# Four rows of each partition of block 4 loaded from GpSimd's queue while the first blocks are stored

## The chip, the cores and the metric

The kernel runs on one core of a Trainium2 chip. The metric is the device time of one execution in microseconds (us); the median of several executions is compared. The core has five engines that run side by side (PE, the matrix engine; DVE, the vector engine; ACT, the scalar engine; POOL, which is GpSimd; SP, the sync engine) and sixteen DMA engines that move data between the chip's main memory (HBM) and the on-chip memory (SBUF, 128 partitions). SP, ACT and GpSimd can each issue transfers on a queue of their own; every transfer is cut up over DMA engines, and each engine that takes part adds to the transfer's semaphore when its part has landed. Sixteen means that all has landed.

## The reference

The computation is a linear layer with a weight that is normalised by column (DoRA). x is 16 x 2048 x 256, so 32768 rows of 256 numbers; all inputs and outputs are float32.

```python
W_adapted = W + scale * (lora_A @ lora_B)                 # 256 x 256, rank 16
W_norm = np.sqrt(np.sum(W_adapted ** 2, axis=0, keepdims=True) + 1e-8)
W_final = W_adapted / W_norm * m
y = x.reshape(-1, 256) @ W_final
```

32 MiB of x are read and 32 MiB of y are written. The weights are small.

## The kernel before, in words

The 32768 rows are eight blocks of 4096. A block lies in SBUF as 128 partitions of 32 rows (1 KB a row), so that a partition's part of a block is one run of 32 KB in HBM. There are five block buffers (`x_bufs`, `XBUFS = 5`): blocks 0 to 4 have a buffer each, and blocks 5 to 7 reuse the buffers of blocks 0 to 2, once those have been stored. Results are written back in place: the product of a piece of x overwrites that piece, and the store reads from the same buffer.

The unit of work is the group `g`: four rows of each partition (`J = 4`), so eight groups make a block (`CH = 8`), and there are 64 groups. Two groups make a pair `p`, 32 in all. For each pair, GpSimd casts x to bf16 (L208), PE transposes it (L321), DVE copies the transposes out of PSUM (L248), PE multiplies by the final weight (L335), and ACT copies each group's product back into the x buffer (L276).

Transfers follow two lists that are written out by hand, `loads` and `stores`, whose entries are (first group, number of groups, rows of each partition in one transfer), with the group after which a store is due as a fourth number. `transfer` (issuing line L146) issues an entry:

- SP issues all loads in the order of the list. Blocks 0 to 3 come first, then 24 of the 32 rows of block 4, all of it in the first 5 us. Then SP waits for store 0 to land, issues the last 8 rows of block 4 as two transfers of four rows, and goes on with two loads of half a block each for block 5. It waits for store 1 before the second half of the sequence (block 6), and for stores 2 and 3 before block 7.
- ACT issues the stores. Store 0 (block 0) is due only after group 19, store 1 (block 1) after group 20, stores 2 and 3 (block 2, 12 and 20 rows) after group 24. The stores of block 3's first five groups are cut in five transfers of four rows; the later ones are larger again.
- GpSimd issues no transfer. At pair 15 (`REST = 15`) it waits until store 2 has landed, before it casts on. PE, DVE and ACT depend on its casts, so that they rest too.

At a cast GpSimd waits for the load that brings the pair's groups, but only where the group before came with another load. A partition's rows of a load or store form one run of bytes, so a load of 24 rows moves runs of 24 KB, one of 4 rows runs of 4 KB.

H is the first group of block 5 (40), so `H - CH` is the first of block 4 (32). At the end, SP waits for the late stores, which closes the program (L360).

Of the kernel before, what the change touches and what calls it, by code (L numbers as in the profile page):

```python
# [11 lines left out]
def kernel(  # L12
# [10 lines left out]
    nc = tc.nc  # L23
    P = 128
# [5 lines left out]
    x_flat = x.flatten_outer_dims()  # L30
    out_flat = out.flatten_outer_dims()
    N, IN = x_flat.shape
# [3 lines left out]
    J = 4  # L36
    DJ = 32
# [5 lines left out]
    XBUFS = 5  # L43
    CH = DJ // J
# [4 lines left out]
    NXB = 2  # L49

    REST = 15
    NXT = 2
    F8 = 2 * J * P

# [7 lines left out]
    def sb(name, shape, dtype):  # L62
        return ctx.enter_context(nc.sbuf_tensor(name, shape, dtype))
# [4 lines left out]
    x_bufs = [sb(f"x_sb{k}", [P, DJ, IN], FP32) for k in range(XBUFS)]  # L68
    xb_bufs = [sb(f"xb{k}", [P, 2 * J, IN], BF16) for k in range(NXB)]
    xt_bufs = [sb(f"xt{k}", [P, F8, KC], BF16) for k in range(NXT)]  # L70
    w_nat = sb("w_nat", [P, KC, OUT], FP32)
# [38 lines left out]
    H = XBUFS * CH  # L110
    loads = [(0, 2, 2 * J), (2, 2, 2 * J), (4, 4, 4 * J)]
    loads += [(b * CH, CH, CH * J) for b in range(1, XBUFS - 1)]
    loads += [(H - CH, 6, 6 * J), (H - 2, 2, J)]
    loads += [(g0, 4, 4 * J) for g0 in range(H, NCH, 4)]
    load_of = {g: n for n, (g0, cnt, _) in enumerate(loads) for g in range(g0, g0 + cnt)}
    stores = [(b * CH, CH, CH * J, 19 + b) for b in range(F - 1)]
# [7 lines left out]
    def pieces(entry):  # L124

        return 16 * (entry[1] * J // entry[2])
# [5 lines left out]
    def sem(name):  # L132
        if name not in sems:
            sems[name] = tc.alloc_semaphore(name)
        return sems[name]

    def transfer(engine, name, entry, dram, store):
        g0, cnt, rows = entry[:3]
        b, c = divmod(g0, CH)
        (u0, ucnt), = [u for u in units if u[0] <= g0 < u[0] + u[1]]  # L140
        unit = dram[u0 * J * P : (u0 + ucnt) * J * P].rearrange("(p j) k -> p j k", p=P)
        for r in range(0, cnt * J, rows):
            here = x_bufs[b % XBUFS][:, c * J + r : c * J + r + rows, :]
            there = unit[:, (g0 - u0) * J + r : (g0 - u0) * J + r + rows, :]
            src, dst = (here, there) if store else (there, here)
            engine.dma_start(out=dst, in_=src).then_inc(sem(name), 16)  # L146

    def load_x(n):
        transfer(nc.sync, f"load{n}", loads[n], x_flat, False)

    def store_y(n):
        transfer(nc.scalar, f"store{n}", stores[n], out_flat, True)

    def wait_load(engine, g):
        engine.wait_ge(sem(f"load{load_of[g]}"), pieces(loads[load_of[g]]))

    def wait_store(engine, n):
        engine.wait_ge(sem(f"store{n}"), pieces(stores[n]))
# [3 lines left out]
        out=w_nat[:], in_=W.rearrange("(p t) o -> p t o", t=KC)  # L162
    ).then_inc(sem("load_w"), 16)
    nc.scalar.dma_start(
        out=a_nat[:], in_=lora_A.rearrange("(p t) r -> p t r", t=KC)
# [2 lines left out]
    nc.scalar.dma_start(out=m_row[:], in_=m[None, :]).then_inc(sem("load_m"), 16)  # L168
    for n in range(len(loads)):

        if loads[n][0] == H - 2:
            wait_store(nc.sync, 0)
        if loads[n][0] == H + CH:
            wait_store(nc.sync, 1)
        if loads[n][0] == H + 2 * CH:
            wait_store(nc.sync, 2)
            wait_store(nc.sync, 3)
        load_x(n)
# [5 lines left out]
        out=identity[:],  # L184
        in_=zeros[:],
# [7 lines left out]
    for p in range(1, NPR):  # L193
        b, c = divmod(p, PRB)
        for g in (2 * p, 2 * p + 1):
            if g == 2 or load_of[g - 1] != load_of[g]:
                wait_load(nc.gpsimd, g)


        if p == 1:  # L200
            nc.gpsimd.wait_ge(sem("dve"), 6)
        if p == 2:
            nc.gpsimd.wait_ge(sem("dve"), 8)
        if p == REST:
            wait_store(nc.gpsimd, FIRST - 2)
        if p >= NXB:
            nc.gpsimd.wait_ge(sem("turned"), p - NXB + 1)
        nc.gpsimd.tensor_copy(  # L208
            out=xb_bufs[p % NXB][:],
            in_=x_bufs[b % XBUFS][:, 2 * c * J : 2 * (c + 1) * J, :],  # L210
        ).then_inc(sem("rounded"), 1)
# [14 lines left out]
        out=wa[:], in0=ab_ps, scalar=float(scale), in1=w_nat[:], op0=ALU.mult, op1=ALU.add  # L226
# [19 lines left out]
    for p in range(NPR):  # L246
        nc.vector.wait_ge(sem("turned"), p + 1)
        nc.vector.tensor_copy(  # L248
            out=xt_bufs[p % NXT][:].rearrange("p r t -> p (r t)").bitcast(FP32),
            in_=xt_ps[p % 2][:],  # L250
# [4 lines left out]
    for engine, idle in ((nc.gpsimd, 8), (nc.vector, 24)):  # L255
# [13 lines left out]
        out=norm[:], in_=n2_ps, func=AF.Sqrt, bias=eps_col[:]  # L269
    ).then_inc(sem("act"), 1)  # L270
    drains = 0
    for g in range(NCH):
        b, c = divmod(g, CH)
        nc.scalar.wait_ge(sem("product"), g + 1)

        nc.scalar.copy(  # L276
            out=x_bufs[b % XBUFS][:, c * J : (c + 1) * J, :], in_=y_ps[g % 2][:]
        ).then_inc(sem("room"), 1)
        due = [n for n in range(len(stores)) if stores[n][3] == g]
        if due:  # L280
            drains += 1
            nc.scalar.drain().then_inc(sem("done"), 1)  # L282
            nc.scalar.wait_ge(sem("done"), drains)
            for n in due:
                store_y(n)
# [42 lines left out]
    def product(p):  # L328
        take("copied")
        for h in range(2):  # L330
            take("room")
            for t in range(KC):
                for j in j_order:
                    r = (h * J + j) * P
                    i = nc.tensor.matmul(  # L335
                        y_ps[h][:, j, :],
                        xt_bufs[p % NXT][:, r : r + P, t],
                        w_final[:, t, :],
# [57 lines left out]
```

## Time and profile before

| what | us |
|---|---|
| median of 9 runs | 162.9 |
| lowest and highest of them | 162.46, 163.8 |
| the profiled execution's own time | 163.03 |
| its span, first to last instruction | 161.7 |
| PE busy | 96.9 |
| ACT busy | 66.0 |
| GpSimd busy | 60.7 |
| DVE busy | 45.0 |
| DMA, mean over the span | 417 GB/s, 67.43 MB |
| GpSimd's wait for store 2 | 23.5 |

The span is that of the program's instructions on the core; 1.3 us of the profiled execution's time lie outside it. Busy times are sums over the span. In the rows of DMA queues, q1 is SP's and q10 is ACT's. The profile also gives, for each of 40 slices of the span, how busy the sixteen DMA engines were on average, and its trace keeps every DMA packet (queue, start, length, bytes) and the time of every semaphore step, without the number of the DMA engine.

### The profile page before, as it was taken

What the parts mean: (1) busy time and instruction counts of PE and PEld (TensorE: products, weight loads), DVE (VectorE), ACT (ScalarE), POOL (GpSimd) and SP (SyncE); (2) the same over time, 40 slices, a digit from 0 to 9 for tenths busy, and PEclk for the clock granted to TensorE, in tenths of its full rate; (3) what the DMA queues carried; (4) which work ended last, traced back from release to release, by engine and by line L of the source; (5) the groups of instructions that cost most, each with busy time, mean ns of one, the idle gap of its engine ahead of it and who ended that gap; (6) DMA issues with size and microseconds to landing.
All of it is one profiled execution on the core that took longest, in us unless ns stands there. A gap on an engine that the chain in (4) does not pass through costs nothing. (4 is left out here: it accounts for less than half of the span.)

```text
span 161.7 us, 2027 instructions
## 1 busy us (share of the span) xinstructions
PE 96.9 (60%) x786; PEld 84.8 (52%) x786; DVE 45.0 (28%) x44; ACT 66.0 (41%) x68; POOL 60.7 (38%) x38
## 2 busy tenths in 40 slices
PE   1596936999997940000899999999895940000000
PEld 0285925899996920000789999878775930000000
DVE  0567321245353330000334444443442300000000
ACT  3321740576866560000067777577572850000000
POOL 1045319476776000003955944944909300000000
PEclk9999995799999995555599999999999998555555
DMA  4999999999999999989999999999999999999994
GB/s 164 420 454 462 389 502 405 389 511 397 421 389 486 389 502 410 438 363 443 392 422 419 412 444 431 414 440 433 413 468 411 470 415 405 472 413 413 430 425 199
DMA packets 4645, 67.43 MB, mean 417 GB/s; under 512 B 657, under 2 KB 674, under 8 KB 1698
## 3 DMA queue, kind: packets, MB, share of 16 engines
q1 hardware_dynamic: 2304, 33.82, 49.0%
q10 hardware_dynamic: 2338, 33.59, 48.9%
q14 instruction: 3, 0.02, 0.0%
HBM read 33.85 MB, written 33.55 MB: 417 GB/s over the span
## 5 line engine op out<-in xcount | busy, mean ns | idle before, releaser
L276 ACT COPY x_sb<-y_ps 128x1024 f32<-128x1024 f32 x64 | 62.2, 1014 | 60.0 <-PE y_ps L335 57.4
L208 POOL CAST xb<-x_sb 128x2048 bf16<-128x2048 f32 x31 | 58.2, 1893 | 65.0 <-DMA x_sb<-in_x_dram 30.7
L335 PE MATMUL y_ps<-w_final,xt 128*128 128x256 bf16 x512 | 64.2, 280 | 4.2 <-PEq L311 4.2
L248 DVE COPY xt<-xt_ps 128x1024 f32<-128x1024 f32 x32 | 39.1, 1224 | 76.3 <-PE xt_ps L321 76.2
L335 PEld LDWEIGHTS y_ps<-w_final,xt 128*128 128x128 bf16 x512 | 51.3, 101 | 12.1 <-issue 5.4
L321 PE MATMUL xt_ps<-identity,xb 128*128 128x128 f32 x264 | 37.7, 291 | 24.9 <-PEq L311 24.7
L321 PEld LDWEIGHTS xt_ps<-identity,xb 128*128 128x128 f32 x264 | 32.5, 151 | 27.1 <-issue 26.6
L264 ACT CAST xb<-x_sb 128x2048 bf16<-128x2048 f32 x1 | 1.9, 1898 | 2.7 <-DMA x_sb<-in_x_dram 2.7
L292 PE MATMUL y_ps<-identity,a_nat 128*16 128x128 f32 x2 | 0.6, 394 | 3.5 <-DMA a_nat<-in_lora_A_dram 3.5
L262 ACT ACT_TABLE_LOAD x1 | 1.3, 1283 | 2.4 <-issue 2.4
L238 DVE RECIPROCAL rnorm<-norm 128x256 f32<-128x256 f32 x1 | 1.8, 1754 | 1.3 <-ACT norm L268 1.3
L305 PE MATMUL y_ps<-sq,ones 128*128 128x256 f32 x4 | 2.1, 674 | 0.0
L292 PEld LDWEIGHTS y_ps<-identity,a_nat 128*16 128x16 f32 x2 | 0.1, 88 | 3.5 <-issue 3.5
L301 PE MATMUL y_ps<-m_row,ones 1*128 1x256 f32 x2 | 1.2, 710 | 1.1 <-DMA m_row<-in_m_dram 1.1
L214 POOL MEMSET xb<- 128x2048 bf16 x1 | 1.8, 1804 | 0.0
L305 PEld LDWEIGHTS y_ps<-sq,ones 128*128 128x128 f32 x4 | 1.2, 326 | 0.8 <-DVE sq L229 0.7
L301 PEld LDWEIGHTS y_ps<-m_row,ones 1*128 1x128 f32 x2 | 0.5, 308 | 1.6 <-DMA m_row<-in_m_dram 1.6
L220 DVE CAST b_bf<-b_nat 16x256 bf16<-16x256 f32 x1 | 0.3, 282 | 2.8 <-DMA b_nat<-in_lora_B_dram 2.8
L268 ACT ACTIVATE norm<-y_ps,eps_col 128x256 f32<-128x256 f32 x1 | 0.5, 474 | 1.2 <-PE y_ps L305 1.2
L296 PE MATMUL y_ps<-b_bf,aT 16*128 16x256 bf16 x2 | 0.6, 404 | 0.6 <-DVE aT L222 0.6
L225 DVE SCALAR_TENSOR_TENSOR wa<-y_ps,w_nat 128x512 f32<-128x512 f32 x1 | 0.7, 692 | 0.8 <-PE y_ps L296 0.8
L241 DVE TENSOR_TENSOR w_final<-wam,rnorm 128x256 bf16<-128x256 f32 x2 | 0.8, 421 | 0.0
(14 smaller groups left out, 3.7 us busy)
## 6 DMA issues: line engine op xcount, KB each, us to landing
out_dram<-x_sb ACTq DMA_DIRECT2D x5, 4096.0 KB, 28.6
x_sb<-in_x_dram SPq DMA_DIRECT2D x7, 2048.0 KB, 30.6
x_sb<-in_x_dram SPq DMA_DIRECT2D x3, 4096.0 KB, 30.1
out_dram<-x_sb ACTq DMA_DIRECT2D x2, 2048.0 KB, 29.4
x_sb<-in_x_dram SPq DMA_DIRECT2D x1, 3072.0 KB, 46.1
out_dram<-x_sb ACTq DMA_DIRECT2D x2, 1536.0 KB, 19.4
out_dram<-x_sb ACTq DMA_DIRECT2D x1, 2560.0 KB, 29.6
out_dram<-x_sb ACTq DMA_DIRECT2D x5, 512.0 KB, 36.9
```

Of the source, the lines that this page charges most:

```text
L208: nc.gpsimd.tensor_copy(out=xb_bufs[p % NXB][:], in_=x_bufs[b % XBUFS][:, 2 * c * J : 2 * (c + 1) * J, :],).then_inc(sem("rounded"), 1)
L214: nc.gpsimd.memset(xb_bufs[NPR % NXB][:], 0.0).then_inc(sem("rounded"), 1)
L238: nc.vector.reciprocal(out=rnorm[:], in_=norm[:]).then_inc(dv, 1)
L241: i = nc.vector.tensor_mul(out=w_final[:, t], in0=wam[:, t], in1=rnorm[:])
L248: nc.vector.tensor_copy(out=xt_bufs[p % NXT][:].rearrange("p r t -> p (r t)").bitcast(FP32), in_=xt_ps[p % 2][:],).then_inc(sem("copied"), 1)
L262: nc.scalar.activation(out=warm[:], in_=eps_col[:], func=AF.Sqrt)
L264: nc.scalar.copy(out=xb_bufs[0][:], in_=x_bufs[0][:, 0 : 2 * J, :]).then_inc(sem("early"), 1)
L276: nc.scalar.copy(out=x_bufs[b % XBUFS][:, c * J : (c + 1) * J, :], in_=y_ps[g % 2][:]).then_inc(sem("room"), 1)
L301: nc.tensor.matmul(mb_ps, ones[0:1, :], m_row[:], start=True, stop=True).then_inc(pe, 1)
L305: i = nc.tensor.matmul(n2_ps, ones[:], sq[:, t, :], start=(t == 0), stop=(t == KC - 1))
L321: i = nc.tensor.transpose(xt_ps[p % 2][:, j * P : (j + 1) * P], xb_bufs[p % NXB][:, j, :].bitcast(FP32), identity[:],)
L335: i = nc.tensor.matmul(y_ps[h][:, j, :], xt_bufs[p % NXT][:, r : r + P, t], w_final[:, t, :], start=(t == 0 and (j % (J // 2)) == 0), stop ...
```

## The change

The load of block 4 is shortened from 24 rows of each partition to 20. The next four rows (20 to 23) are loaded by GpSimd, in three transfers that are issued just before its wait at pair 15: one for partitions 0 to 5, one for partitions 6 to 125, one for partitions 126 and 127 (`SHARES`). The last eight rows are loaded by SP as before, as two transfers of four rows behind its wait for store 0, now with the semaphore `short`. GpSimd waits for `side` and `short` in full before it casts pair 18, whose second group holds rows 20 to 23; before, there was no wait at pair 18, and the eight rows were waited for at pair 19. The groups 37 to 39 are in no entry of `loads` any more, hence the guard with `in load_of`.

```diff
+    SIDE = 4
+    SHORT = 4
+    SHARES = ((0, 6), (6, 120), (126, 2))
...
-    loads += [(H - CH, 6, 6 * J), (H - 2, 2, J)]
+    loads += [(H - CH, 5, 5 * J)]
...
+    def load_end(engine, name, p0, cnt, r, rows, **kw):
+
+        unit = x_flat[(H - CH) * J * P : H * J * P].rearrange("(p j) k -> p j k", p=P)
+        engine.dma_start(
+            out=x_bufs[XBUFS - 1][p0 : p0 + cnt, r : r + rows, :],
+            in_=unit[p0 : p0 + cnt, r : r + rows, :],
+            **kw,
+        ).then_inc(sem(name), 16)
...
-        if loads[n][0] == H - 2:
+        if loads[n][0] == H:
             wait_store(nc.sync, 0)
+            for r in range(5 * J + SIDE, DJ, SHORT):
+                load_end(nc.sync, "short", 0, P, r, SHORT)
...
-            if g == 2 or load_of[g - 1] != load_of[g]:
+            if g in load_of and (g == 2 or load_of.get(g - 1) != load_of[g]):
                 wait_load(nc.gpsimd, g)
...
         if p == REST:
+            for k, (p0, cnt) in enumerate(SHARES):
+                load_end(
+                    nc.gpsimd, "side", p0, cnt, 5 * J, SIDE, max_dma_last_dim=SIDE * IN
+                )
             wait_store(nc.gpsimd, FIRST - 2)
+        if 2 * p < H - 3 <= 2 * p + 1:
+            nc.gpsimd.wait_ge(sem("side"), 16 * len(SHARES))
+            nc.gpsimd.wait_ge(sem("short"), 16 * ((3 * J - SIDE) // SHORT))
```

GpSimd's program gains the three transfers; the instructions of the other engines, and their order, are the same, but for the widths of SP's loads of block 4.

## The prediction

> **What bounds the kernel now.** I read the page first (DMA rows, queues, chain that ended last), then busy time by stage, then the order of time around the change, then the DMA issues, and last the trace's records of single DMA packets and of each semaphore's sixteen landings.
>
> ```profile
> span 161.7 us, 2027 instructions
> DMA  4999999999999999989999999999999999999994
> q1 hardware_dynamic: 2304, 33.82, 49.0%
> q10 hardware_dynamic: 2338, 33.59, 48.9%
> PE y_ps L335 3%; PE xt_ps L321 2%; ACT x_sb L276 1%; ACTq L282 1%
> ```
>
> The two queues (q1: loads from SP; q10: stores from ACT) fill 97.9% of sixteen engines' span. The chain of instructions is short, because the last 29 us hold none: only stores drain. So the time is the bytes at the DMA engines' rate, plus any moment in which an engine has nothing to do, plus the lateness of the engine that ends last. By stages (the last two columns are the DMA share and GB/s):
>
> ```profile
> 12.90:47.70 34.80, 29.29 (x246) 26.32 (x246) 13.59 (x12) 19.37 (x20) 20.93 (x12) 0.90 1.00 433
> 60.00:75.50 15.50, 0.00 (x0) 0.00 (x0) 0.00 (x0) 0.89 (x1) 0.00 (x0) 0.54 0.99 422
> 75.50:90.00 14.50, 12.43 (x96) 11.10 (x97) 4.90 (x4) 6.49 (x7) 10.29 (x6) 0.79 1.00 414
> 140.00:159.00 19.00, 0.00 (x0) 0.00 (x0) 0.00 (x0) 0.00 (x0) 0.00 (x0) 0.50 1.01 434
> 159.00:160.00 1.00, 0.00 (x0) 0.00 (x0) 0.00 (x0) 0.00 (x0) 0.00 (x0) 0.50 0.31 131
> 160.00:161.00 1.00, 0.00 (x0) 0.00 (x0) 0.00 (x0) 0.00 (x0) 0.00 (x0) 0.50 0.12 49
> 161.00:161.70 0.70, 0.00 (x0) 0.00 (x0) 0.00 (x0) 0.00 (x0) 0.00 (x0) 0.50 0.00 0
> ```
>
> One queue alone runs at 433 to 434 GB/s; loads and stores mixed, at 422 and 414. From 160 to 161 us the share is 0.12, about two engines of sixteen: two are late, and the span waits for them. The packet records say how late. Each engine has eight packets per full transfer and then a 4-byte packet for the semaphore; on one engine the next packet starts 3 to 4 ns before the last one ends, so each engine's sequence can be followed. The last semaphore packets end at 159.4 to 160.2 us on fourteen engines, at 160.79 on one (the second late engine) and at 161.36 on one (the late engine). The late engine was level with the others at 49.6 us, 0.6 us behind at 69.7, 1.3 at 84 and 1.7 at the end. The second got its 1.15 in two stores of 32 KB packets: 0.37 at 49 to 60 us, 0.48 at 123.8 to 131.5 (six packets of 1.27 to 1.32 us where 1.213 is usual), the rest in pieces.
>
> ```profile
> 47.74 0.37 ACTq L146 DMA_DIRECT2D out_dram<-x_sb  x1
> 50.11 1.90 POOL L208 CAST xb<-x_sb 128x2048 bf16<-128x2048 f32 x1 [0.73 <-PE xt_ps L321]
> 75.53 3.73 POOL L208 CAST xb<-x_sb 128x2048 bf16<-128x2048 f32 x2 [23.53 <-DMA out_dram<-x_sb]
> 83.31 1.89 POOL L208 CAST xb<-x_sb 128x2048 bf16<-128x2048 f32 x1 [1.84 <-PE xt_ps L321]
> 60.06 26.78 SPq L146 DMA_DIRECT2D x_sb<-in_x_dram  x8
> ```
>
> Store 0 is issued at 47.74. GpSimd ends pair 14 at 52.0 and then sits 23.5 us for store 2. Pair 18 is cast at 83.31. SP issues nothing between 4.7 and 60.06, where store 0 has landed.
>
> ```profile
> x_sb<-in_x_dram SPq DMA_DIRECT2D x1, 3072.0 KB, 46.1
> out_dram<-x_sb ACTq DMA_DIRECT2D x1, 4096.0 KB, 12.3
> out_dram<-x_sb ACTq DMA_DIRECT2D x1, 2048.0 KB, 29.3
> ```
>
> The load that the change shortens lands 46.1 us after its issue (50.34 us): it is the last thing in q1. The last store waits: its issue is 29.3 us before its landing and it needs 4.9, so some 24 us lie between compute and the end.
>
> **The change part by part.**
>
> *Load of block 4: 20 rows in place of 24.* Per engine eight packets of 24 KB (0.916 us each) become eight of 20 KB (0.763, between that and the 0.761 of 20 KB stores): 1.22 us less in q1. Engines ended this load at 49.45 to 49.88 us (median 49.62) and passed straight to store 0. They will end it at 48.24 to 48.67, median 48.40.
>
> *The join to store 0.* Store 0's issue doesn't move: its products come from blocks 0 to 2. When can its first packet start? The row: the first ACT issue began at 0.90 us, on empty rings, and its first packet started at 1.93, 1.03 us later; so 47.74 + 1.03 = 48.77. Every engine is then idle from its end of load to 48.77: 0.37 us at the median. The Trainium skill, "DMA: Bandwidth & Descriptors", Specifications, gives about 0.6 us to the first byte for the hardware path: store 0 could start at 48.35, and the hole closes to nothing at the median. I take the trace's 1.03; the other end stays for the range. After the join all engines start together, 0.89 us earlier than before at the median, 0.88 on the late engine, 0.69 on the second (it ended its load at 49.46).
>
> *Three transfers on GpSimd.* They issue after pair 14, at 52.0, and lie in the 23.5 us wait, so GpSimd pays nothing for them; with some us per issue they would still fit. If that cover were gone, compute would move by it, and has the 24 us above. Their 128 pieces of 4 KB cost 0.159 us each (4 KB loads of before). Spread evenly that is 8 x 0.159 = 1.27 per engine against 1.22 saved: +0.05, and three semaphore packets of 0.009. The sum over all engines is kept; what changes is who does it. No queue of GpSimd's is in the trace. The skill (same page, "Why a DMA increments its semaphore by 16 and not by 1") says that a GpSimd transfer is cut over the largest count up to 16 that divides its outer size, on consecutive engines from a cursor that goes round. With the cursor at engine 0 at the start: 6 partitions go to engines 0 to 5, 120 go as 15 shares of 8 to engines 6 to 15 and 0 to 4, 2 go to 5 and 6. Engine 5, the sixth, gets 2 pieces and the others 8 or 9. The same section states an exception, direct copies that use sixteen shares with partitions/16 rounded up: then 120 partitions fill engines 0 to 14, and it is the sixteenth that is spared. I take the first, since only it fits what the shares 6, 120, 2 add up to; the second is a rival.
>
> Ends of the engines, against before:
> - the late engine, if it is the sixth: 161.36 - 0.88 + 2 x 0.159 + 0.03 = 160.83
> - the second: 160.79 - 0.69 + 8 or 9 x 0.159 + 0.03 = 161.40 to 161.56
> - a typical one: 159.6 - 0.89 + 1.30 to 1.46 = 160.0 to 160.2.
>
> So the second late engine ends last: +0.04 to +0.20 us against 161.36. Had store 0 started at 48.35 this would be -0.3 to -0.2.
>
> *A third queue beside the stores.* SP's first short load was issued at 60.06 and had its first packet at 64.15[...]; so GpSimd's begin near 57 and, one 0.159 packet after each 1.213 one, last eight or nine turns of 1.37: to about 69. Before, mixing began at 64. Seven more microseconds mixed, at the price of the row of 60 to 75.5 (422 for 433, 2.5%), is 0.18 us; the row of 75.5 to 90 (414, 4.4%) would make 0.31, and small packets read beside large writes may cost nothing, as 90 to 121 us ran at 435: 0 to 0.31, and I take 0.1.
>
> *The moved waits.* The two short loads still follow store 0, on SP, as many and as large (512 KB each); store 0 starts 0.89 earlier and carries two or three extra packets, so SP moves by -0.5 us or so. The new wait at pair 18 is for GpSimd's and the short loads. Before, the short loads landed at 73.1 and 79.4; pair 18 is cast at 83.31: 4 us of cover. Behind that wait are all later casts, and behind them PE, ACT and the stores; without cover it would eat of the 24 us and not lengthen the run.
>
> Sum: +0.04 to +0.20, plus 0.1: **+0.2 us**. Made on the profiled execution (span 161.7, own time 163.03), which is 0.13 over the median of 162.9: so 163.1. A run of this kernel can be told from no change from about 0.3%, 0.49 us.
>
> **The rivals.**
>
> *A: the share misses the late engine.* By the exception, because the cursor stands elsewhere at launch, or because the late engine isn't the sixth. The late engine then takes 8 or 9 pieces too: 161.36 - 0.88 + 1.30 to 1.46 = 161.78 to 161.94, +0.4 to +0.6, with mixing +0.5 to +0.7: slower, 163.4 to 163.6. The trace numbers no engines, so nothing in it says that the late one is the sixth; it decides as soon as fewer than about 3 pieces are spared there. For: the hole at the join is paid by all. Against: by the cursor rule the shares spare exactly one engine, and the trace has one that is later than all the others.
>
> *B: the third queue stalls the engines.* The trace has such stalls where stores and loads are mixed: at 68.3 three packets of 1.213 took 1.34, 1.62 and 1.74, and the 20 KB stores of 77 to 84 us lost 6.8 us together, 0.42 per engine. A second such episode and slow descriptors of GpSimd: +0.8 to +1.5, 163.7 to 164.4. Against: at 90 to 121 us mixing costs nothing.
>
> *C: faster.* The second engine's lateness is one execution's accident, and the late engine's is not: the stalls of the second come in two stores alone. Then the late engine ends last at 160.83, with mixing 160.9: -0.4; with store 0's first packet at 48.35 as well, -0.8. 162.1 to 162.5. For: the fastest run of before is 162.46, so lateness does vary.
>
> **How the numbers follow.** My forecast 0.42, A 0.27, B 0.10, C 0.21. Within 0.3% lie 0.32 of the forecast, 0.05 of A and 0.02 of C: 0.39. Slower: 0.07 of the forecast, 0.22 of A, B: 0.39. Faster: 0.03 of the forecast and 0.19 of C: 0.22. Range 162.2 to 164.0: it leaves out the best of C and the worst of B. The forecast's own range is 162.6 to 163.5.
>
> **What would show it.** Right: a dip of the DMA row at 48.3 to 48.8 us; a third queue of about 0.52 MB between 57 and 70; pair 18 still held by PE and not by a DMA; after 159 us one or two engines left over, with less than the 2.0 us (159.38 to 161.36) that lie between the first ender and the last before. Wrong: no dip (C's half); an engine that still ends 1.5 us after the others (A); a new stretch below 415 GB/s at 57 to 75 us (B); the span below 161.2 or above 162.2.

## The result, and the profile after

The changed kernel takes 163.79 us (median of 10 executions, 163.26 to 164.16), the kernel before 162.89 (31 executions). The ratio is 1.0055, with a 95% interval of 1.0041 to 1.0070: slower by about 0.9 us. Timed once more beside other kernels it was 163.91 against 162.74, ratio 1.0079 (1.0053 to 1.0106).

The execution with the profile was one of the longer ones of this kernel, 164.9 us. So I read three traces of the changed kernel: this one, a second (163.89) and a third (163.72). From the page of the first (DMA busy, rates, queues; q0 is GpSimd's):

```profile
span 163.6 us, 2030 instructions
DMA  4999998999999999989999999999999999999992
DMA packets 4853, 67.43 MB, mean 412 GB/s; under 512 B 737, under 2 KB 754, under 8 KB 1906
q10 hardware_dynamic: 2338, 33.59, 48.8%
q1 hardware_dynamic: 2304, 33.29, 47.8%
q0 software_dynamic: 208, 0.52, 0.8%
```

The bytes are the same and the engines are as busy, but they moved 412 GB/s in place of 417. There is no dip at 48 us. The stages (last columns: DMA share, GB/s) say where the rate went:

```profile
12.90:47.70 34.80, 29.27 (x252) 26.61 (x253) 14.33 (x12) 19.44 (x21) 21.70 (x12) 0.95 1.01 434
52.00:60.00 8.00, 5.16 (x46) 4.29 (x44) 2.45 (x2) 4.76 (x5) 1.20 (x2) 0.99 1.02 426
60.00:75.50 15.50, 0.00 (x0) 0.00 (x0) 0.00 (x0) 0.00 (x0) 0.00 (x0) 0.50 0.98 404
75.50:90.00 14.50, 10.98 (x80) 9.64 (x81) 3.67 (x3) 5.42 (x6) 9.41 (x5) 0.72 1.01 412
160.00:161.00 1.00, 0.00 (x0) 0.00 (x0) 0.00 (x0) 0.00 (x0) 0.00 (x0) 0.50 0.35 147
161.00:162.00 1.00, 0.00 (x0) 0.00 (x0) 0.00 (x0) 0.00 (x0) 0.00 (x0) 0.50 0.15 66
162.00:163.00 1.00, 0.00 (x0) 0.00 (x0) 0.00 (x0) 0.00 (x0) 0.00 (x0) 0.50 0.12 49
```

Up to 47.7 us the rate does not differ. In 60 to 75.5 us it is 404 GB/s where it was 422; the third trace has 404 too, but the second has 424, and its execution was as long as the median:

```profile
60.00:75.50 15.50, 0.00 (x0) 0.00 (x0) 0.00 (x0) 0.00 (x0) 0.00 (x0) 0.50 1.01 424
```

So the lower rate of this stage is not the whole loss. At the end a tail of two engines (share 0.12) lasts until 163, two microseconds later than before. In order of time around the change:

```profile
46.98 0.37 ACTq L152 DMA_DIRECT2D out_dram<-x_sb  x1
51.18 2.03 POOL L160 DMA_DIRECT2D x_sb<-in_x_dram  x3
76.98 3.73 POOL L234 CAST xb<-x_sb 128x2048 bf16<-128x2048 f32 x2 [23.78 <-DMA out_dram<-x_sb]
85.16 1.89 POOL L234 CAST xb<-x_sb 128x2048 bf16<-128x2048 f32 x1 [2.24 <-PE xt_ps L347]
```

GpSimd's three issues take 2.0 us and lie ahead of its wait for store 2, which still is 23.8 us long; pair 18 is held by PE (2.24 us) and by no DMA, as forecast. The end of a run can be told by two numbers, both from the sixteen landings of the last store (one from each DMA engine): their median, and the last. How far the last is behind the median is called lateness here.

| execution | span | median landing | last landing |
|---|---|---|---|
| before | 161.7 | 159.98 | 161.69 |
| after, first trace | 163.6 | 160.81 | 163.56 |
| after, second trace | 162.6 | 160.13 | 162.55 |
| after, third trace | 162.4 | 160.87 | 162.37 |

Against the one trace of before, the first has +0.83 in the median (all engines slower) and +1.04 in lateness. In the second nearly all is lateness (+0.15 and +0.71), in the third all is in the median (+0.89, lateness 1.50 for 1.71). So the loss seems to have two forms that come in different shares. Single traces can't fix the shares: in the kernels below that lose nothing that can be told, the median landing lies between 159.90 and 160.55 and the lateness between 1.0 and 1.4.

### The profile page after: what moved, and what is told of

It reads as the page before. It is cut to its first block, busy times and chain, and to the rows that moved or that the text cites. A ratio compares the mean times of both kernels' runs of the same rounds, so it can differ in the third digit from the quotient of the medians.

```text
span 163.6 us, 2030 instructions
## 1 busy us (share of the span) xinstructions
PE 96.1 (59%) x786; PEld 84.2 (51%) x786; DVE 45.0 (28%) x44; ACT 66.0 (40%) x68; POOL 62.6 (38%) x41
## 5 line engine op out<-in xcount | busy, mean ns | idle before, releaser
L347 PE MATMUL xt_ps<-identity,xb 128*128 128x128 f32 x264 | 37.2, 289 | 27.4 <-PEq L337 27.4
L347 PEld LDWEIGHTS xt_ps<-identity,xb 128*128 128x128 f32 x264 | 32.2, 150 | 29.6 <-issue 29.1
L160 POOL DMA_DIRECT2D x_sb<-in_x_dram x3 | 2.0, 680 | 0.0
```

What stands on the lines that cost most here:

```text
L160: engine.dma_start(out=x_bufs[XBUFS - 1][p0 : p0 + cnt, r : r + rows, :], in_=unit[p0 : p0 + cnt, r : r + rows, :], **kw,).then_inc(sem(na ...
L347: i = nc.tensor.transpose(xt_ps[p % 2][:, j * P : (j + 1) * P], xb_bufs[p % NXB][:, j, :].bitcast(FP32), identity[:],)
```

## The experiments

Two theories stood at the start. M: engines lose time wherever small loads stand beside large stores, whoever issues them. S: the loss is GpSimd's queue itself. Ratios are to the kernel before on the same chip, with 95% intervals; they are not quotients of medians. "Pieces" are the 4 KB packets of the moved rows.

### Same moment, SP's queue

```diff
+            nc.sync.wait_ge(sem("go"), 1)
+            load_end(nc.sync, "side", 0, P, 5 * J, SIDE)
             wait_store(nc.sync, 0)
...
-            for k, (p0, cnt) in enumerate(SHARES):
-                load_end(
...
+            nc.gpsimd.sem_inc(sem("go"), 1)
...
```

> The four rows go as one transfer of 128 partitions on SP's queue, at the moment at which GpSimd issued them (GpSimd signals SP). Theory M (engines lose time whenever small loads stand beside the large stores, whoever issues them): no gain over the changed kernel, 163.6 to 164.0. Theory S (the loss is GpSimd's queue itself: its descriptors and its 16-byte packets): back to 162.8 to 163.1.

163.07 us, ratio 1.0021 (1.0007 to 1.0035). Most of the loss is gone, but not all: some 0.3 us remain for four more rows of 4 KB pieces beside stores 0 and 1 (M), and about 0.6 us go with the queue that issues them (S). The run also makes one transfer of the three; the next run shows that this does not matter.

### Even shares

```diff
-    SHARES = ((0, 6), (6, 120), (126, 2))
+    SHARES = ((0, P),)
```

> GpSimd issues one transfer of all 128 partitions, eight pieces for each engine and none spared. If the spared engine gains from being spared (six pieces of 0.159 us), this is slower than the changed kernel by up to 0.9 us, 164.0 to 164.7. If the engine that ends last is another one, as the trace of the changed kernel suggests (it has nine pieces), this is the same or up to 0.2 us faster: 163.5 to 163.9. M and S say the same of it.

163.74 us, ratio 1.0072 (1.0040 to 1.0104): not to be told from the changed kernel. The eight executions spread from 162.81 to 164.75. The one with the profile was the shortest, and in it the stores lost next to nothing at 57 to 70 us (0.02 us per engine). The loss beside stores is thus no fixed price: some executions escape it. To spare one engine is worth nothing that this shows.

### The four rows on SP, behind the 20

```diff
+            load_end(nc.sync, "side", 0, P, 5 * J, SIDE)
             wait_store(nc.sync, 0)
...
-            for k, (p0, cnt) in enumerate(SHARES):
-                load_end(
...
```

> The four rows are loaded by SP right behind the 20 rows, beside no store. M and S both say that the loss goes: 162.8 to 163.1, the time of the kernel before (the same bytes up to store 0, in 4 KB pieces for the last four rows). If the loss came from cutting block 4's load (more packets, another start of store 0), it would stay near 163.7.

162.98 us, ratio 1.0007 (0.9996 to 1.0017). Cutting block 4's load costs nothing that can be told; what costs is where and from whom the four rows come.

### Never three queues

```diff
             wait_store(nc.sync, 0)
+            nc.sync.wait_ge(sem("side"), 16 * len(SHARES))
```

> The changed kernel, but SP's short loads also wait until GpSimd's rows have landed, so that never three queues run at once (two at any time). If it is the third queue that stalls the engines: 163.0 to 163.3. If two queues do it as well (M): 163.6 to 164.0. What it adds: SP's later loads start some 12 us later, which the store backlog covers.

163.57 us, ratio 1.0057 (1.0037 to 1.0078), in six executions: as slow as the changed kernel. A third queue is not needed for the loss.

### Twice the rows on GpSimd

```diff
-    SIDE = 4
+    SIDE = 8
...
-    max_dma_last_dim=SIDE * IN
+    max_dma_last_dim=4 * IN
```

> GpSimd loads eight rows in place of four (pieces of 4 KB still, twice as many), SP's short load is one transfer of four rows in place of two. If GpSimd's pieces cost each (theory S, per piece): the loss over the kernel before doubles, to about 1.8 us: 164.4 to 164.8. If the queue costs once, however much it carries: 163.5 to 163.9. If small pieces beside stores cost the same from any queue (M), the number of them beside stores is 24 an engine in both: 163.5 to 163.9 as well.

164.10 us, ratio 1.0080 (1.0060 to 1.0100), beside 163.91 and 1.0079 for the changed kernel timed with it. No further 0.9 us came; the 0.2 us between the medians are within the noise of six executions each. The median lies between the two expectations and meets neither. SP has one short transfer less here, so that as many small pieces stand beside the stores as before.

### A token on GpSimd's queue

```diff
         if p == REST:
+            nc.gpsimd.dma_start(out=token[:], in_=m[None, :]).then_inc(sem("token"), 16)
             wait_store(nc.gpsimd, FIRST - 2)
+        if p == REST + 3:
+            nc.gpsimd.wait_ge(sem("token"), 16)
```

(added to the kernel before, with a tile `token`)

> The kernel before, whose loads all stay with SP, and GpSimd issues one transfer of 1 KB at pair 15 (m into a tile that nothing reads) and waits for it at pair 18. If a GpSimd queue costs once, by being there: 163.2 to 163.6. If it costs by what it carries: 162.7 to 163.0.

162.93 us, ratio 1.0007 (0.9994 to 1.0020). The queue costs nothing that can be told by being there.

### GpSimd's rows beside loads

```diff
+        if p == 4:
+            for k, (p0, cnt) in enumerate(SHARES):
+                load_end(
...
         for g in (2 * p, 2 * p + 1):
...
-            for k, (p0, cnt) in enumerate(SHARES):
-                load_end(
...
             wait_store(nc.gpsimd, FIRST - 2)
```

> GpSimd issues its three transfers before pair 4, about 18 us, so that they run beside SP's loads of blocks 1 and 2 and beside no store. If the loss needs stores beside GpSimd's pieces: 162.7 to 163.1. If GpSimd's pieces cost in any company: 163.4 to 163.9. Block 1 lands up to 1.2 us later, which by itself moves store 0's issue and no more.

165.23 us, ratio 1.0144 (1.0122 to 1.0166). I expected this run to be free or to lose as much as the changed kernel; it lost 2.5 us. It is the clearest of all: no store runs at that time.

### The same rows beside the same loads, ACT's queue

```diff
-            for k, (p0, cnt) in enumerate(SHARES):
-                load_end(
...
+        if g == 1:
+            load_end(nc.scalar, "side", 0, P, 5 * J, SIDE)
```

> The four rows as one transfer of 128 partitions on ACT's queue, issued after group 1 (about 17.5 us), so beside SP's loads of blocks 1 and 2, as GpSimd's were in the run that lost 2.5 us. If any second queue of small loads slows the large ones: 164.5 to 165.4, with 32 KB load packets of 1.4 to 1.5 us from 20 to 36 us. If that slowing is GpSimd's queue alone (S): 162.6 to 163.1, with packets of 1.21 us.

162.75 us, ratio 1.0007 (0.9994 to 1.0021): no loss. The stage from 18 to 36 us of three kernels, in this order: before, GpSimd's rows beside loads, ACT's rows beside loads (last columns: DMA share, GB/s):

```profile
18.00:36.00 18.00, 13.84 (x106) 12.04 (x104) 5.33 (x5) 8.57 (x9) 9.06 (x5) 0.81 0.99 426
```

```profile
18.00:36.00 18.00, 13.00 (x102) 11.44 (x101) 5.34 (x5) 8.14 (x9) 9.06 (x7) 0.81 1.01 371
```

```profile
18.00:36.00 18.00, 13.38 (x110) 12.00 (x108) 5.22 (x5) 8.96 (x10) 9.00 (x5) 0.91 0.99 424
```

The engines are busy in all three (share 0.99 to 1.01), but with GpSimd's pieces among the loads they move 371 GB/s. The packet records say how: while pieces of q0 are in flight (21.4 to 36.5 us) SP's 154 packets of 32 KB take 1.476 us on average; at all other times they take 1.218. The pieces themselves are short (median 0.168). 154 x (1.476 - 1.213) / 16 engines = 2.5 us, the whole loss.

It can be pinned down further by following each engine's packets in order. An SP packet right behind one of GpSimd's pieces took 1.49 us on average (125 packets, none under 1.34); behind another SP packet it took 1.22, and behind one of ACT's pieces, in the other kernel, 1.216 (112 packets, 20.2 to 29.1 us). Behind a 16-byte packet of GpSimd's queue it still took 1.39, so the 4 KB are not what costs. All sixteen engines have it alike (means of 1.46 to 1.49), so the uneven shares are not the cause. That GpSimd's queue slows the packets of another queue beside loads is shown here; why it does is not.

### The changed kernel again, and its third trace

No edit.

> The changed kernel once more, on the chip of the other three of this job, for its time beside theirs and a second trace: 163.6 to 164.0. If the lateness of single engines is what costs, the trace has again two or three engines that end over 1.5 us behind the median; if it was one execution's accident, fewer or none.

163.91 us, ratio 1.0079 (1.0053 to 1.0106). In the second trace three engines land 1.5 us or more behind the median (1.5, 1.8 and 2.4).

> The changed kernel, one execution more with a trace: 163.3 to 164.7. If its loss is mainly lateness of single engines, the last of the sixteen ends of the last store is again 1.5 us or more behind their median and the spared engine is one of the late ones; if it is mainly a lower rate of all, the median itself is late by 0.8 us or more.

163.72 us, one execution. The last engine is 1.5 us behind a median that is itself 0.89 late, and the spared engine is not late: this is the lower rate of all. The second trace has the other form.

One thing orders the traces, the moment at which store 0 was issued. It goes with PE's granted clock from 18 to 36 us: at 0.99 to 1.00 store 0 came at 45.3 us (six traces), at 0.89 to 0.91 at 46.8 to 47.2, at 0.81 at 47.7 and later. The rates from 60 to 75.5 us, in GB/s:

| store 0 issued, us | GpSimd's rows not beside the stores | beside them |
|---|---|---|
| 46.8 to 47.7 | 422 (before), 419 (SP's queue), 422 (ACT, beside loads), 415 (the small start below) | 404, 404 (changed, first and third trace), 388 (twice the rows) |
| 45.3 | 424 (SP, behind the 20), 420 (token) | 424 (changed, second trace), 428 (even shares), 426 (never three queues), 420 (the eleventh spared, below) |

With a late store 0 the stage is slower where GpSimd's rows run, and slower still with twice as many; with an early one it is not. The early start has a price of its own: the stores then begin beside the last loads, and an engine loses 0.4 to 0.9 us on average at 44 to 49 us, with GpSimd's rows or without (0.6 in the trace of the token, 0.9 in that of SP's rows behind the 20). These are single traces, and the timed executions do not tell the moment of store 0, so this is a pattern and not a cause that was tested.

### Another engine spared

```diff
-    SHARES = ((0, 6), (6, 120), (126, 2))
+    SHARES = ((0, 11), (11, 105), (116, 12))
```

> The changed kernel with shares of 11, 105 and 12 partitions. By the rule of consecutive engines they give the eleventh engine two pieces in place of the sixth, and the others 8 or 9. If it matters that the late engine is the spared one, this is slower than the changed kernel, by up to 0.9 us: 164.2 to 164.8. If what is spared is worth nothing: 163.5 to 164.0. In the trace, the spared engine is the one whose pieces are replaced by 16-byte packets: if stalls at 60 to 80 us follow those packets, it is again a late one; if they belong to a fixed engine, it is not.

163.35 us, ratio 1.0038 (1.0021 to 1.0056): not slower than the changed kernel, rather less slow. No gain from sparing the sixth engine rather than the eleventh is seen. The traces suggest why sparing pays little. An engine that has no piece of a transfer gets a 16-byte packet for each piece that each of the others gets, and in three traces its store packets of 32 KB grew meanwhile:

| trace | spared engine, 32 KB store packets beside its 16-byte packets, us | the others, mean and median |
|---|---|---|
| after, first | 1.29, 1.38, 1.40, 1.51, 1.38, 1.38, 1.36, 1.87 | 1.27, 1.23 |
| after, third | 1.22, 1.38, 1.41, 1.44, 1.50, 1.34, 1.32, 1.86 | 1.27, 1.23 |
| eleventh spared | 1.21, 1.21, 1.41, 1.44, 1.58, 1.51 | 1.22, 1.21 |

The six pieces spared are worth 0.95 us; the spared engine of the first trace gave back 1.8 us in these eight packets (their sum less 8 x 1.213) and ended 1.6 behind the median; that of the third ended level with it. In the second trace it begins only at 64 us (1.30, 1.61, 1.34), once the short loads have joined, and with the shorts held back it doesn't occur before its last packet (1.38). So it goes with being spared; if the cut follows the cursor rule (below), the spared engine was another one in the last row. Whether the 16-byte packets cause it or the engine's being ahead of the others does, these runs don't say.

### A small start of store 0

```diff
-    stores = [(b * CH, CH, CH * J, 19 + b) for b in range(F - 1)]
+    stores = [(0, 2, J, 19), (2, CH - 2, (CH - 2) * J, 19)]
+    stores += [(b * CH, CH, CH * J, 19 + b) for b in range(1, F - 1)]
```

(in the kernel before; the waits for stores are renumbered)

> The kernel before, with store 0 begun by two transfers of four rows (4 KB pieces) ahead of its other 24 rows. In several traces every engine loses 0.4 to 1.1 us at 46 to 49 us, where 32 KB stores begin beside the last large loads, while 4 KB stores beside 16 KB loads lose nothing from 90 to 115 us. If small pieces at the start avoid the first: 162.2 to 162.6. If it is the start of any store beside large loads: 162.7 to 163.0.

163.04 us, ratio 1.0012 (0.9995 to 1.0029): no gain. In its trace 0.31 us per engine are lost at 57 to 70 us and 0.51 at 70 to 85, where the trace of before has 0.09 and 0.44. Whether the small start helps against the loss at 46 to 49 us its trace can't tell, since store 0 came at 47.1 in it, and with so late a store 0 the trace of before loses nothing there either. No version here beats the kernel before.

## Why the prediction was right, and where not

The range held, but the forecast of +0.2 us did not: +0.9 was measured. Two of its terms failed, the price of mixing and the lateness at the end; that the number fell into the range is luck as far as they go.

- **Load of block 4.** Right. Engines ended the 20-row load at 48.20 to 48.56 us; 48.24 to 48.67 was forecast.
- **The hole at the join.** It didn't occur in the trace. The step that failed is "store 0's issue doesn't move": it came at 46.98 us, not 47.74, and the first store packet followed the load's last at 48.22. Nothing of the change lies ahead of it. PE's granted clock from 18 to 36 us was 0.91 for 0.81, and at 0.99 to 1.00 the issue came at 45.3. Moments of compute vary between executions by over two microseconds. The 0.37 us were not paid in this trace, so other terms cost more than the total shows.
- **GpSimd's transfers.** Issues (2.0 us) and the wait at pair 18 cost nothing, as forecast; GpSimd's rows had landed at 72.6, the short loads at 80.2. The first packet came at 56.8 (57 forecast), the last at 72.3 and not 69: the 16-byte and the semaphore packets wait behind store packets as well as the pieces do. The cut follows the cursor rule of the Trainium skill ("DMA: Bandwidth & Descriptors", "Why a DMA increments its semaphore by 16 and not by 1"): the 208 packets of q0 are 128 pieces, 48 semaphore packets and 32 of 16 bytes (10 + 8 + 14). All sixteen engines send a semaphore packet for each of the three transfers, also those without a piece. One engine has two pieces, six have nine, nine have eight. By the exception some engine would have ten pieces and one none; the first two traces show neither. The trace has no engine numbers, so whether the late engine of before is the sixth stays open; it hardly matters, as even shares and the eleventh spared are not slower.
- **The end.** The step that failed is to take the late engine of before for one that is always late. Rival C called the second late engine the accident; it is the other way round. In all fourteen traces one engine lost 0.5 to 0.7 us at about 120 to 132 us, as the second did before. But in the traces of the token, of SP's rows behind the 20 and of ACT's rows beside loads that engine ends last (1.0 to 1.2 us behind the median), and no other is more than 0.6 behind: an engine 1.7 us late, which the shares were made to spare, isn't there. In the changed kernel engines with nine pieces end last (2.8 and 2.3 us behind the median in the first trace), through stalls at 48 to 85 us that the sum didn't have.
- **The mixing.** This is the term that was mis-sized: 0.1 us taken, 0 to 0.31 allowed. Measured, the timed runs give 0.3 us for four rows on SP's queue and 0.9 for GpSimd's. In the first and third traces the stage of 60 to 75.5 us alone lost (422 - 404) / 422 x 15.5 = 0.66 us of rate; in the second it lost none, and the loss is in late engines. I priced it by stages in which SP's and ACT's queues alone run. I also misread one of them: "small packets read beside large writes may cost nothing" was taken from 90 to 121 us, but there 4 KB stores stand beside 16 KB loads, the other way round. The nearest rule ("DMA: Bandwidth & Descriptors", "Issuing engines are not separate DMA queues") says that transfers of all queues run on the same sixteen engines and interleave. That is so, but interleaving was not free: 371 GB/s for 424 beside loads.
- **The chances.** Rival B, a third queue that stalls the engines, was nearest (0.8 to 1.5 us forecast, 0.9 measured), at a chance of 0.10. Its mechanism was half right: not the third queue does it but GpSimd's, with two queues too. The range of 162.2 to 164.0 held 163.79 because B's lower part and rival A lay in it; the forecast's own range ended at 163.5.

Open: why twice the rows cost hardly more, whether the moment of store 0 is why the loss beside stores varies so between executions (162.81 to 164.75 with even shares) where that beside loads varies less (164.51 to 165.44), and what in GpSimd's queue slows the others.

## What to carry to other kernels

Where the DMA engines are the bound, a transfer moved to GpSimd's queue need not be neutral even if GpSimd is idle (here it cost 0.9 us beside stores and 2.5 beside loads): price the slower packets of the other queues, not only its own, and try the same transfer at the same moment on a hardware queue before shaping its shares. And read the end of a DMA-bound kernel as two numbers, the median engine's end and the last one's: a cure for the late engine that slows the median or makes another engine late is lost. Before curing a late engine, see in a second trace whether it is late again.

## What the runs showed of the hardware that I had not expected

- While GpSimd's pieces were in flight beside SP's loads, a 32 KB load packet took 1.476 us on average for 1.218 otherwise; behind ACT's pieces it took 1.216. The packet right behind a GpSimd piece was the slow one (1.49).
- An engine that takes no part in a GpSimd transfer still gets a packet of 16 bytes for each piece that the others get; with even shares there were none (144 packets in q0 in place of 208).
- GpSimd's first packets started 5.6 us after its first issue beside stores (51.18 to 56.79, first trace) and 3.9 us beside loads (17.51 to 21.36).
- One engine lost 0.5 to 0.7 us at about 120 to 132 us in each of the fourteen traces.
- Where store 0 began beside the last loads (issued at 45.3 us), an engine lost 0.4 to 0.9 us on average at 44 to 49 us; where it was issued at 46.8 us or later, it lost 0.03 at most.
